# First post-norm of the prompt's first half: columns 0 to 256 normed between the projection tiles of columns 256 to 512, with six split weights kept

## The chip, the cores and the metric

One core of a Trainium2 chip runs the whole program. The metric is the device time of one execution in microseconds. TensorE (PE) does the matrix products, and its weight loads (PEld) run beside them. VectorE (DVE), ScalarE (ACT) and GpSimd (POOL) do the elementwise work, and SyncE (SP) issues most of the transfers between HBM and the chip's memory. Products accumulate in PSUM banks; other tiles lie in SBUF. Every engine has its own queue and takes its instructions in the order in which they stand there.

## The reference

One layer of a streaming encoder, for 1024 prompt frames and 32 sample frames (1056 columns together) of width 1024, in float32:

```
h = x * (1 + sc1) + sh1                    # sc1, sh1, g1 ... from silu(c) @ w_ada
mq, mk, mv, mo, mi, mf, fq, fk, fv, ff, gu, gv = split(h @ w_in)
hm = mlstm(mq, mk, mv, mi, mf) ; hf = forgetting_attention(fq, fk, fv, ff)
vn = layer_norm(gv)                        # also an output for the sample frames
hg = gu * (tril(ws) @ vn + bs)             # per chunk of 128 frames
mix = concat(hm, hf, hg) @ w_o
x = layer_norm(ALPHA * x + (1 + g1) * mix, ln1_g, ln1_b)
h = x * (1 + sc2) + sh2
y = (silu(h @ w_gate) * (h @ w_up)) @ w_down
x = layer_norm(ALPHA * x + (1 + g2) * y, ln2_g, ln2_b)
```

The keys, values and gates of the attention and the states of the mLSTM are outputs too.

## The kernel before

**Arithmetic.** Activations lie with the model dimension on the 128 partitions (8 slices, called k) and frames as columns. Each float32 product is made of three matmuls on halves of the operands: high by high (L117), low by high (L118) and high by low (L119). A weight tile is loaded (`raw`), cast on ACT to its high half (`whi`, L105), and subtracted on VectorE for the low half (`wlo`, L106).

**Columns.** Group 0 is frames 0 to 512, group 1 the other 544 columns. The norm of group 0 works on two ranges of it, `MM[0]`: columns 0 to 256 and 256 to 512.

**The stage that matters here** comes after the mLSTM and the prompt's attention for group 0:

1. `wo_mix(0, ...)` loads the mixers' outputs from HBM (`start_dmix`) into `mlstm_al`, casts the high half into `mlstm_ah` on ACT (L997) and leaves the low half in `mlstm_al`. Six slices are asked for before the gMLP's units, the last two after. `wo_res(0)` loads the residual into `wo_z`, one transfer for each of 8 slices.
2. Four `tm_unit` calls compute the gMLP's halves `gv` and `gu`. `evac_gv` norms `gv` and stores it to HBM (`start_dvn`); a spatial product (L723) takes it back as `tm_gvn`. The gMLP's output is transposed on PE into one bank of the pool `tm_g` (L731) and copied out by ACT as `tm_gms` (L733). Two kinds of FoX unit share PE's `g` banks with it: `fm_unit` computes the attention's queries and keys for one head (`fm_g`, evacuated at L366, L367 and L368 into `fm_qkh`, `fm_qkl`, `fm_qkr`).
3. `wo(0, st, (cut,), ...)` runs once for each range: 8 output tiles (m), each of 8 slices by three matmuls 128x256. Each run loads, casts and splits its own 8 weights. `sublayer_end` evacuates a tile at L1046 on VectorE; `less()` (L1041, POOL) takes off a pivot, the first tile's column mean; `ln_sum` adds the tile into `wo_zs` on POOL (L939) and its square, made by ACT, into `wo_qs` on VectorE (L941).
4. Then `ln1` norms range 0 and after it range 1: two matmuls sum `wo_zs` and `wo_qs` over the partitions (L951), some short VectorE instructions make the scale r and the shift e (L960 to L973), and for each slice there are a multiply (L1063), an add (L1064, on POOL for two of eight), ACT's scale and shift into `lna_tmp` (L1067), ACT's cast into `mlstm_ah` (L1071), and VectorE's low half (L1072). These halves are the operands of the feed-forward's up projection (`up_g`).
5. The last FoX units follow, then `ln1_res` scales the normed residual on POOL (L1081), and the sample's attention `fox_sample` (`foxs_...`, L908 for its output) and the up projections begin.

**What sets the order.** The code is written in this order, but a scheduler places every instruction by a simulated timeline, so instructions of the last FoX units and of the first up projection stand between those of the two norms. A tile waits for its buffer: a pool with n buffers of one tag lets n be alive. PE's accumulators `tm_g`, `fm_g`, `wo_g` and the first `up_g` come from one pool of three banks. `mlstm_ah` and `mlstm_al` of group 0 lie in tiles `ah` and `al` of the pool `ph`; the modulated input of group 0 lies in tiles of its own, `start_h1h` and `start_h1l`, in the pool `p1a`, which is closed (`s6`) once the last FoX unit that reads group 0 has run.

## Time and profile before

| | |
|---|---|
| median of 3 runs | 1378.0 us (1377.67 to 1381.36) |
| profiled execution | 1383.65 us, span of its trace 1381.0 us |
| mean granted TensorE clock | 0.991 |
| gMLP units, first FoX units | up to about 378 us |
| output projection of group 0 (`wo_g`), its matmuls | 378.5 to 425.2 us |
| norms of its two ranges (their sums over partitions, to the last low half) | 425.3 to 471 us |
| group 1, feed-forward, final norms | to the end |

Times in the trace count from the start of its span. A row of the timeline gives start, length, engine, line, operation, output and inputs, and in brackets how long the engine had been idle and what ended it. In a timeline row the length of a matmul includes its way through the pipeline, so rows overlap. In the table of stretches the columns are the stretch, its length, the busy time (and the instructions) of PE, of weight loads, VectorE, ACT and POOL, the granted TensorE clock as a share of full speed, the mean busy share of the 16 DMA engines, and GB/s.

### The profile page before, as it was taken

To read this page: it belongs to the slowest core of one execution; us is meant where nothing else is said; L and a number is where in the kernel's file an instruction comes from. 1 tells how busy PE (TensorE), PEld (TensorE's weight loads), DVE (VectorE), ACT (ScalarE), POOL (GpSimd) and SP (SyncE) were. 2 spreads that over 40 slices of the span, in tenths; PEclk is the share of its full clock that TensorE was granted. 3 is DMA by queue.
4 is the path that set the end of the run, shared out by engine and by line. 5 is a ranking of instruction groups with operands and counts; after the bars stand their busy time and mean duration, and the time that the engine had idled before them with its cause. 6 is when DMAs were issued, how large, how long until landed. Compare 5 with 4: busy or idle time off the path is not lost.

```text
span 1381.0 us, 25237 instructions
## 1 busy us (share of the span) xinstructions
PE 1340.4 (97%) x9432; PEld 1222.8 (89%) x9432; DVE 1008.3 (73%) x2144; ACT 653.7 (47%) x1274; POOL 242.6 (18%) x272
## 2 busy tenths in 40 slices
PE   7999999999899799999999999999999999999996
PEld 4898889889899678888887889899999999999996
DVE  5545654688678757777776766668998988888777
ACT  3314454444445444545544455435564554545355
POOL 0202000033167400000000000264610000000341
PEclk9999999999999999999999999999999999999999
DMA  9765554554764765553443433664597768463321
GB/s 362 261 234 152 162 187 151 175 160 121 244 185 143 212 178 157 139 144 117 135 121 101 105 116 96 192 176 128 156 238 194 206 160 221 131 176 119 98 90 65
DMA packets 123545, 224.65 MB, mean 163 GB/s; under 512 B 21292, under 2 KB 66264, under 8 KB 123424
## 3 DMA queue, kind: packets, MB, share of 16 engines
q1 hardware_dynamic: 117984, 212.75, 49.9%
q0 software_dynamic: 5296, 10.16, 4.7%
q8 instruction: 74, 1.21, 0.4%
q14 instruction: 47, 0.39, 0.1%
q10 hardware_dynamic: 144, 0.14, 0.0%
HBM read 191.21 MB, written 51.72 MB: 176 GB/s over the span
## 4 chain that ended last, share of the span: by engine, by line
PE 84%; DVE 8%; DMA 3%; ACT 2%; issue 1%; POOL 0%; SPq 0%; DVEq 0%; ACTq 0%; POOLq 0%
PE up_g L117 5%; PE up_g L118 5%; PE up_g L119 5%; PE dn_g L119 4%; PE dn_g L117 4%; PE dn_g L118 4%; PE sup_u L119 3%; PE sup_u L117 3%; PE sup_u L118 3%; PE tm_g L283 2%; PE tm_g L282 2%; PE tm_g L284 2%; PE wo_g L119 2%; PE wo_g L117 2%; PE wo_g L118 2%; PE fox_t L818 2%
## 5 line engine op out<-in xcount | busy, mean ns | idle before, releaser
L117 PE MATMUL up_g<-mlstm_ah,up_whi 128*128 128x512 f32 (+1 forms) x384 | 141.8, 370 | 5.0 <-ACT lna_tmp L1067 3.3
L118 PE MATMUL up_g<-mlstm_al,up_whi 128*128 128x512 f32 (+1 forms) x384 | 142.2, 370 | 0.6 <-DVE mlstm_al L1072 0.6
L119 PE MATMUL up_g<-mlstm_ah,up_wlo 128*128 128x512 f32 (+1 forms) x384 | 141.3, 368 | 0.0
L283 PE MATMUL tm_g<-tm_wlo,start_h1h 128*128 128x256 f32 (+1 forms) x384 | 109.5, 286 | 0.9 <-DVE tm_wlo L106 0.9
L282 PE MATMUL tm_g<-tm_whi,start_h1h 128*128 128x256 f32 (+1 forms) x384 | 109.4, 287 | 0.2 <-DVE tm_traw L352 0.2
L284 PE MATMUL tm_g<-tm_whi,start_h1l 128*128 128x256 f32 (+1 forms) x384 | 109.3, 286 | 0.0
L1191 ACT CAST sup_whi<-sup_raw 128x1024 fp32r<-128x1024 f32 x54 | 56.0, 1047 | 90.7 <-PE dn_u L118 47.2
L117 PEld LDWEIGHTS up_g<-mlstm_ah,up_whi 128*128 128x128 f32 x384 | 73.4, 191 | 17.3 <-ACT mlstm_ah L1071 3.5
L118 PEld LDWEIGHTS up_g<-mlstm_al,up_whi 128*128 128x128 f32 x384 | 73.5, 191 | 12.4 <-DVE up_actl L1125 0.8
L119 PEld LDWEIGHTS up_g<-mlstm_ah,up_wlo 128*128 128x128 f32 x384 | 73.7, 192 | 10.8
L791 ACT ACTIVATE fox_p<-fox_s,fox_fmx 128x384 f32<-128x384 f32 (+2 forms) x96 | 55.2, 579 | 56.4 <-DVE fox_fmx L789 43.4
L105 ACT CAST up_whi<-up_raw 128x1024 fp32r<-128x1024 f32 x50 | 52.4, 1048 | 60.8 <-PE dn_g L118 20.6
L1046 DVE SCALAR_TENSOR_TENSOR wo_z<-dn_g,start_mod,wo_z 128x512 f32<-128x512 f32 (+4 forms) x120 | 60.2, 520 | 22.2 <-PE dn_g L119 21.5
L1192 DVE TENSOR_TENSOR sup_wlo<-sup_raw,sup_whi 128x1024 fp32r<-128x1024 f32 x54 | 68.1, 1265 | 10.8 <-ACT sup_whi L1191 10.8
L283 PEld LDWEIGHTS tm_g<-tm_wlo,start_h1h 128*128 128x128 f32 x384 | 72.2, 188 | 2.5 <-issue 1.2
L282 PEld LDWEIGHTS tm_g<-tm_whi,start_h1h 128*128 128x128 f32 x384 | 72.1, 189 | 2.1 <-issue 0.8
L106 DVE TENSOR_TENSOR up_wlo<-up_raw,up_whi 128x1024 fp32r<-128x1024 f32 x50 | 66.6, 1333 | 9.6 <-ACT up_whi L105 8.9
L117 PE MATMUL dn_g<-up_acth,dn_whi 128*128 128x512 f32 (+2 forms) x200 | 73.5, 368 | 0.0
L118 PE MATMUL dn_g<-up_actl,dn_whi 128*128 128x512 f32 (+2 forms) x200 | 73.3, 368 | 0.0
L119 PE MATMUL dn_g<-up_acth,dn_wlo 128*128 128x512 f32 (+2 forms) x200 | 73.3, 366 | 0.0
L284 PEld LDWEIGHTS tm_g<-tm_whi,start_h1l 128*128 128x128 f32 x384 | 72.2, 188 | 0.9 <-issue 0.8
L105 ACT CAST dn_whi<-dn_raw 128x1024 fp32r<-128x1024 f32 (+1 forms) x44 | 42.7, 971 | 50.6 <-PE up_g L118 11.3
(643 smaller groups left out, 4606.0 us busy)
## 6 DMA issues: line engine op xcount, KB each, us to landing
up_raw<-w_gu SPq DMA_DIRECT2D x50, 512.0 KB
dn_raw<-w_dn SPq DMA_DIRECT2D x28, 512.0 KB
ada_late<-w_ada SPq DMA_DIRECT2D x24, 512.0 KB
wo_raw<-w_o SPq DMA_DIRECT2D x24, 512.0 KB
sup_raw<-w_gu SPq DMA_DIRECT2D x20, 512.0 KB
start_dp<-w_gu SPq DMA_DIRECT2D x19, 512.0 KB
start_dp<-w_gu POOLq DMA_DIRECT2D x19, 512.0 KB, 7.7
sup_raw<-start_dp SPq DMA_DIRECT2D x18, 512.0 KB
```

Source lines behind the costliest of these rows:

```text
L105: nc.scalar.copy(hi[:, :w], raw[:, :w])
L106: (eng or nc.vector).tensor_tensor(lo[:, :w], raw[:, :w], f(hi[:, :w]), ALU.subtract)
L117: nc.tensor.matmul(ps, hi, xh(k), start=start and k == 0, stop=False)
L118: nc.tensor.matmul(ps, hi, xl(k), start=False, stop=False)
L119: nc.tensor.matmul(ps, lo, xh(k), start=False, stop=stop and k == n - 1)
L282: nc.tensor.matmul(ps[:, :ncol], xh, hi, start=k == 0, stop=False)
L283: nc.tensor.matmul(ps[:, :ncol], xh, lo, start=False, stop=False)
L284: nc.tensor.matmul(ps[:, :ncol], xl, hi, start=False, stop=k == 7)
L791: nc.scalar.activation(pr[:, lo:hi], banks[x][:, :hi - lo], AF.Exp, bias=mxs[:, 0:1], accum_out=sums[:, x:x + 1])
L1046: self.lastz = self.nc.vector.scalar_tensor_tensor(z[:, m, x:y], ps[:, x - a:y - a], g[i], z[:, m, x:y], ALU.mult, ALU.add)
L1191: nc.scalar.copy(h, x)
L1192: tt(l, x, f(h), ALU.subtract)
```

## The change

1. Group 0's projection is split. `wo_range` does range 0's eight tiles; then range 1's tiles are made in the order 0, 5, 6, 7, 3, 4, 1, 2, and woven with `ln1` of range 0: one slice of the norm for one tile in the text. The norm of range 1 follows.
2. Six of the eight split weights stay in SBUF for range 1: 0, 1 and 2 in a pool of their own (`pw`), 5, 6 and 7 in the pool where they were made. Weights 3 and 4 are loaded and split again.
3. `ln_begin(nc.vector)`: the sums into `wo_zs` are made on VectorE. The adds of group 0 for k = 1 and 5 (L1064) too.
4. One place for two operands: group 0's modulated input now lies in the same tiles `ah` and `al` that later hold the mixers' outputs; `p1a` and `s6` are gone, and a slice of the mixers' outputs can be loaded once the last reader of the input's slice there is done.
5. `wo_res` loads the residual in two transfers of 1 MB instead of eight of 256 KB.
6. Stores leave SP's queue: the `gv` rows (`start_dvn`, 9 of them) and the keys `o_kT` go to POOL's queue; for the heads after the norm `o_kT` goes to ACT's queue, and the key itself and the sample's queries and keys are made by ACT instead of POOL.
7. The sample's attention output takes 12 matmuls of 32x64 for each group of heads instead of 24 of 64x32, then a copy, a transposing matmul and a copy; its stores, now two for each group, are on ACT's queue.
8. Smaller buffers make room: one `mixs` buffer instead of two, `tmres` in `tmsum`'s place, narrower `late` and kept weights.

```
-    def weights(self, src, nk, ncol, eng=None):
+    def weights(self, src, nk, ncol, eng=None, pool=None):
+        pool, width = (pool, 1024) if pool else (self.wp, 1056)
...
-        self.store(self.dvn[:n, tt, :], v[:n])
+        self.store(self.dvn[:n, tt, :], v[:n], nc.gpsimd)
...
-            nc.gpsimd.tensor_tensor(kr[:, :n], f(hi[:, :n]), f(lo[:, :n]), ALU.add)
+            if act:
+                nc.scalar.activation(kr[64:, :n], ps[64:], AF.Copy)
+            else:
+                nc.gpsimd.tensor_tensor(kr[:, :n], f(hi[:, :n]), f(lo[:, :n]), ALU.add)
...
-            self.store(self.d["o_kT"][h, :, o:o + n], kr[64:, :n])
+            self.store(self.d["o_kT"][h, :, o:o + n], kr[64:, :n], nc.scalar if act else nc.gpsimd)
...
-            for x in range(4):
-                for b in range(3):
-                    nc.tensor.matmul(o[r, oc], vv, pT[:w, b, 32 * x:32 * x + 32], start=b == 0, stop=b == 2)
+            for b in range(3):
+                for x in range(4):
+                    nc.tensor.matmul(o[32 * x:32 * x + 32, 0:64], pT[:w, b, 32 * x:32 * x + 32],
+                                     vc[:, b, h] if b < 2 else self.vs[:, h], start=b == 0, stop=b == 2)
+            nc.scalar.copy(ob, o[:, 0:64])
+            nc.tensor.transpose(o[0:64, P:2 * P], ob, self.ident)
...
-        for k in range(KT):
-            self.load(z[:, k], self.d["xT"][k, :, GO[c]:GO[c] + GN[c]])
+        for k in range(0, KT, 4):
+            self.load(z[:, k:k + 4], self.d["xT"][k:k + 4, :, GO[c]:GO[c] + GN[c]].rearrange("k p n -> p k n"))
...
+    def wo_range(self, st, a, b, order, kept, pool):
+        nc, ko = self.nc, self.KORDER
+        hh, hl = self.hh[0][a], self.hl[0][a]
+        st["order"] = order
+        for m in order:
+            self.phase = "wo0"
+            w = kept.get(m) or self.weights(self.d["w_o"][m], KT, P, None, pool if m < 3 else None)
+            kept[m] = w
+            ps = self.t(self.pg, [P, 512], F32, "g")
+            self.gemm(ps[:, :b - a], [w[k] for k in ko], slice(0, P), lambda i: hh[:, ko[i], :b - a],
+                      lambda i: hl[:, ko[i], :b - a])
+            self.sublayer_end(0, self.z[0], m, ps, "g1", st, a, b)
+            yield
...
-            (nc.gpsimd if k % 4 == 1 else nc.vector).tensor_tensor(zk, zk, e, ALU.add)
+            (nc.gpsimd if c and k % 4 == 1 else nc.vector).tensor_tensor(zk, zk, e, ALU.add)
...
-        self.h1t = [[self.t(p, [P, KT, n], F32R, x) for x in ("h1h", "h1l")] for p, n in zip((p1a, self.p1), GN)]
+        self.h1t = [self.wide_tiles(), [self.t(self.p1, [P, KT, GN[1]], F32R, x) for x in ("h1h", "h1l")]]
...
-        st = self.ln_begin(nc.gpsimd)
-        for cut in MM[0]:
-            self.wo(0, st, (cut,), nc.vector)
-        self.operand(0, self.ph)
-        for a, b in MM[0]:
-            weave(self.ln1(0, st, a, b))
+        st = self.ln_begin(nc.vector)
+        with ExitStack() as s7:
+            pw = self.pool("pw", ctx=s7)
+            kept = {}
+            weave(self.wo_range(st, *MM[0][0], range(KT), kept, pw))
+            del kept[3], kept[4]
+            weave(self.wo_range(st, *MM[0][1], (0, 5, 6, 7, 3, 4, 1, 2), kept, pw), self.ln1(0, st, *MM[0][0]))
+        weave(self.ln1(0, st, *MM[0][1]))
         for h in range(PRE, 8):
-            self.fm_unit(w3[2 + h], self.evac_qk(h), (1,))
+            self.fm_unit(w3[2 + h], self.evac_qk(h, True), (1,))
```

**Where the instructions go.** In the rows below, a name's number tells its instance, `x8` means that many alike in a row, and lines of the kernel after stand a little higher: L1063 becomes L1088, L1064 L1089, L1046 L1071, L951 L960, L939 L948.

TensorE before, at the end of the projection: the rows `wo_g_5400` are the last tile of range 1, and `wo_zs_4836`, `wo_qs_4837` are range 0's sums.

```order
L119 MATMUL wo_g_5400<-mlstm_ah_3907,wo_wlo_5397 128x256
L117 MATMUL wo_g_5400<-mlstm_ah_3907,wo_whi_5396 128x256
L118 MATMUL wo_g_5400<-mlstm_al_3908,wo_whi_5396 128x256
L119 MATMUL wo_g_5400<-mlstm_ah_3907,wo_wlo_5397 128x256
L951 MATMUL lna_t_5431<-wo_zs_4836,start_onesm_138 128x256
L951 MATMUL lna_t_5433<-wo_qs_4837,start_onesm_138 128x256
L117 MATMUL fm_g_5559<-start_h1h_171,fm_whi_5555 128x272
```

TensorE after, at the third tile (`wo_g_5203`) of range 1, whose weight halves `wo_whi_5050` and `wo_wlo_5051` are kept ones:

```order
L119 MATMUL wo_g_5166<-mlstm_al_3901,wo_whi_5013 128x256
L120 MATMUL wo_g_5166<-mlstm_ah_3900,wo_wlo_5014 128x256
L118 MATMUL wo_g_5203<-mlstm_ah_3900,wo_whi_5050 128x256
L933 MATMUL wo_t_5148<-wo_z_755_3920,start_ones_45_140 128x256
L960 MATMUL lna_t_5153<-wo_zs_4820,start_onesm_138 128x256
L119 MATMUL wo_g_5203<-mlstm_al_3901,wo_whi_5050 128x256
L120 MATMUL wo_g_5203<-mlstm_ah_3900,wo_wlo_5051 128x256
```

The sums of range 0 now stand between the matmuls of range 1's third tile, and not behind its eighth.

VectorE before, where range 0's norm begins (`lna_tmp_5435` and `wo_pv_4838` are the statistics of range 0, `wo_g_5400` is the last projection tile):

```order
L1046 SCALAR_TENSOR_TENSOR wo_z_759_3927<-wo_g_5400,start_mod_156,wo_z_759_3927 128x256
L106 TENSOR_TENSOR fm_wlo_5706<-fm_raw_5703,fm_whi_5705 128x1024
L941 TENSOR_TENSOR wo_qs_4837<-wo_qs_4837,wo_tmp_5427 128x256
L970 SCALAR_TENSOR_TENSOR lna_tmp_5435<-lna_t_5433,start_epsa_117,lna_tmp_5435 128x256
L960 SCALAR_TENSOR_TENSOR lna_tmp_5435<-lna_tmp_5435,wo_pv_4838 128x256
L367 SCALAR_TENSOR_TENSOR fm_qkl_5585<-fm_g_5559,start_qsc_147,fm_qkh_5584 128x272
L961 TENSOR_TENSOR lna_tmp_5435<-lna_tmp_5435,wo_pv_4838 128x256
L962 SCALAR_TENSOR_TENSOR wo_pv_4838<-lna_tmp_5435,wo_pv_4838 128x256
L973 SCALAR_TENSOR_TENSOR wo_qs_4837<-lna_t_5431,wo_pv_4838 128x256
L1063 TENSOR_TENSOR wo_z_759_3927<-wo_z_759_3927,wo_pv_4838 128x256 x8
L1064 TENSOR_TENSOR wo_z_759_3927<-wo_z_759_3927,wo_qs_4837 128x256 x3
```

VectorE after, in the middle of range 1's projection (`wo_g_5240`, `wo_g_5283` and `wo_g_5326` are its fourth, fifth and sixth tiles):

```order
L1071 SCALAR_TENSOR_TENSOR wo_z_755_3920<-wo_g_5240,start_mod_156,wo_z_755_3920 128x256
L970 TENSOR_TENSOR lna_tmp_5157<-lna_tmp_5157,wo_pv_4822 128x256
L948 TENSOR_TENSOR wo_zs_4820<-wo_zs_4820,wo_z_755_3920 128x256
L971 SCALAR_TENSOR_TENSOR wo_pv_4822<-lna_tmp_5157,wo_pv_4822 128x256
L107 TENSOR_TENSOR fm_wlo_5508<-fm_raw_5505,fm_whi_5507 128x1024
L982 SCALAR_TENSOR_TENSOR wo_qs_4821<-lna_t_5153,wo_pv_4822 128x256
L1088 TENSOR_TENSOR wo_z_755_3920<-wo_z_755_3920,wo_pv_4822 128x256 x8
L1071 SCALAR_TENSOR_TENSOR wo_z_755_3920<-wo_g_5283,start_mod_156,wo_z_755_3920 128x256
L1089 TENSOR_TENSOR wo_z_755_3920<-wo_z_755_3920,wo_qs_4821 128x256
L107 TENSOR_TENSOR fm_wlo_5583<-fm_raw_5580,fm_whi_5582 128x1024
L1089 TENSOR_TENSOR wo_z_755_3920<-wo_z_755_3920,wo_qs_4821 128x256 x5
```

All eight multiplies of range 0's norm now stand ahead of the evacuation of range 1's fifth tile, and the adds around it and the sixth's.

ScalarE before, at the copy `tm_gms` that frees a bank of PE:

```order
L105 CAST wo_whi_4841<-wo_raw_4839 128x1024
L997 CAST mlstm_ah_3907<-mlstm_al_3908 128x512 x3
L733 COPY tm_gms_4627<-tm_g_4560 128x512
L997 CAST mlstm_ah_3907<-mlstm_al_3908 128x512
L714 COPY tm_vhl_4651<-tm_tmres_4649 32x256
```

ScalarE after:

```order
L1008 CAST mlstm_ah_3900<-mlstm_al_3901 128x512
L106 CAST wo_whi_4828<-wo_raw_4826 128x1024
L106 CAST wo_whi_4865<-wo_raw_4863 128x1024
L106 CAST fm_whi_4730<-fm_raw_4728 128x1024
L296 COPY tm_tmsum_4633<-tm_g_4616 32x256
L1008 CAST mlstm_ah_3900<-mlstm_al_3901 128x512 x2
L740 COPY tm_gms_4613<-tm_g_4546 128x512
```

Two casts of the mixers' outputs instead of three stand right ahead of that copy; the casts of two projection weights stand further ahead of it.

More of the change, by code (lines that the diff above doesn't have):

```diff
@@ L175, in ada @@
         for half in range(2):
-            raw = self.t(pool, [P, 1056], F32, tag, bufs)[:, :1024]
+            raw = self.t(pool, [P, 1024 if tag == "late" else 1056], F32, tag, bufs)[:, :1024]
             self.load(raw, self.d["w_ada"][u, :, half * 1024:(half + 1) * 1024])
@@ L974, in ln_stats, with wide_tiles @@
         return r, e
+    def wide_tiles(self):
+        return [self.t(self.ph, [P, KT * 544], F32R, x, 1)[:, :KT * 512].rearrange("p (k n) -> p k n", k=KT)
+                for x in ("ah", "al")]
     KORDER = (2, 3, 4, 5, 0, 1, 6, 7)
@@ L982, in operand @@
             if 0 not in self.hh:
-                tile = lambda tag: self.t(pool, [P, KT * 544], F32R, tag, 1)[:, :KT * 512].rearrange(
-                    "p (k n) -> p k n", k=KT)
-                self.hh[0], self.hl[0] = ({0: x, 256: x[:, :, 256:]} for x in (tile("ah"), tile("al")))
+                self.hh[0], self.hl[0] = ({0: x, 256: x[:, :, 256:]} for x in self.wide_tiles())
             return
@@ L1343, in run @@
         self.constants()
[L1344 removed]
+        self.ph = self.pool("ph")
+        s1 = ExitStack()
         self.p1 = self.pool("p1", ctx=s1, side="right")
         self.sm = self.pool("sm", 2, ctx=s1, side="right")
[L1347 to L1348 removed]
+        self.h1t = [self.wide_tiles(), [self.t(self.p1, [P, KT, GN[1]], F32R, x) for x in ("h1h", "h1l")]]
         self.hs = self.t(self.p1, [P, KT, 2 * NS], F32R, "hs")
```

36 lines of the change are left out of this document (17 added, 19 removed).

## The prediction

> **What bounds the kernel now.** I read the page's list of busy time first.
>
> ```profile
> span 1381.0 us, 25237 instructions
> PE 1340.4 (97%) x9432; PEld 1222.8 (89%) x9432; DVE 1008.3 (73%) x2144; ACT 653.7 (47%) x1274; POOL 242.6 (18%) x272
> ```
>
> TensorE is busy for 97% of the span; VectorE is busy enough to become late in a stage, POOL is not. A change that leaves the matmuls alone, as this nearly does, is worth only what TensorE waits, and what its clock loses. So next come the waits of TensorE in the stage around the change, 330 to 480 us (columns: waited for, us in total, times, longest), and then the granted clock (before the last two columns) in the stretches behind the waits.
>
> ```profile
> PE up_g L117 <- ACT lna_tmp L1067: 3.3, 1, 3.3
> PE fm_g L117 <- ACT tm_gms L733: 2.6, 1, 2.6
> PE ada_g L179 <- DVE up_sil L1123: 1.9, 1, 1.9
> PE up_g L117 <- DVE fm_qkl L367: 1.3, 1, 1.3
> PE wo_g L117 <- ACT tm_gms L733: 0.9, 1, 0.9
> PE up_g L118 <- DVE mlstm_al L1072: 0.6, 1, 0.6
> PE up_g L117 <- DVE ada_adam L187: 0.3, 1, 0.3
> ```
>
> ```profile
> 365.00:371.00 6.00, 6.00 (x29) 6.00 (x29) 1.63 (x4) 1.53 (x4) 0.76 (x1) 0.52 1.00 356
> 400.00:420.00 20.00, 20.00 (x168) 19.95 (x167) 17.12 (x22) 9.58 (x16) 13.03 (x12) 1.00 0.59 179
> 463.00:467.00 4.00, 3.89 (x21) 3.89 (x22) 2.48 (x7) 3.99 (x11) 4.00 (x8) 0.59 0.46 167
> 470.00:474.00 4.00, 4.00 (x31) 2.98 (x24) 1.66 (x6) 0.37 (x1) 0.00 (x0) 0.61 1.04 208
> ```
>
> The projection (400 to 420 lies in it) runs at full clock, 168 matmuls in 20 us or 0.119 us each. On both sides of it lie two holes. Place A, around 364: 2.6 us of waiting, then a stretch that loses 6.0 x (1 - 0.52) = 2.9 us, 5.5 together. Place B, 451 to 476: the five waits on lna_tmp, up_sil, fm_qkl, mlstm_al and ada_adam, 3.3 + 1.9 + 1.3 + 0.6 + 0.3 = 7.4 us, and 4 x 0.41 + 4 x 0.39 = 3.2 us of lost clock, 10.6 together. Some 16 us are therefore to be had, and not more.
>
> Why A waits is in the timelines of TensorE, ScalarE and SP's queue.
>
> ```profile
> 364.58 0.60 PE L117 MATMUL fm_g<-start_h1h,fm_whi 128*128 128x272 f32 x1 [2.62 <-ACT tm_gms L733]
> ```
>
> ```profile
> 358.93 0.62 ACT L997 CAST mlstm_ah<-mlstm_al 128x512 fp32r<-128x512 f32 x1 [2.79 <-DMA mlstm_al<-start_dmix]
> 361.32 1.04 ACT L105 CAST wo_whi<-wo_raw 128x1024 fp32r<-128x1024 f32 x1
> 362.26 1.65 ACT L997 CAST mlstm_ah<-mlstm_al 128x512 fp32r<-128x512 f32 x3
> 363.94 0.59 ACT L733 COPY tm_gms<-tm_g 128x512 f32<-128x512 f32 x1
> ```
>
> ```profile
> 355.16 2.71 SPq L87 DMA_DIRECT2D mlstm_al<-start_dmix  x6
> 357.91 6.23 SPq L87 DMA_DIRECT2D wo_z<-xT  x8
> ```
>
> The copy that frees PE's bank starts at 363.94, behind a weight cast and three casts of mixer outputs, and the first of these casts itself stood 2.79 us waiting for its load. Those six loads leave SP only at 355.16, with the residual's eight right behind them.
>
> Why B waits is in VectorE's rows for the two norms.
>
> ```profile
> 428.48 0.47 DVE L970 SCALAR_TENSOR_TENSOR lna_tmp<-lna_t,start_epsa,lna_tmp 128x256 f32<-128x256 f32 x1
> ...
> 448.56 0.47 DVE L970 SCALAR_TENSOR_TENSOR lna_tmp<-lna_t,start_epsa,lna_tmp 128x256 f32<-128x256 f32 x1
> ```
>
> The first norm's statistics begin at 428.48, the second's only at 448.56, 20 us later; the waits at B are TensorE standing until the second delivers.
>
> **The change part by part.** The sum is made against the profiled execution, 1383.65 us, which lies 5.65 above the median of 1378.0; I take the difference for both and subtract it from the median.
>
> *The weave of norm and projection.* The sums over partitions of range 0 move from behind all 192 matmuls of range 1 to behind 49 of them: 143 x 0.119 = 17 us earlier. VectorE isn't free then, so what counts is when it has done both jobs. Its prices are in its groups for 376 to 475 us (instructions, busy us, mean ns), with those of POOL behind.
>
> ```profile
> L106 DVE TENSOR_TENSOR wo_wlo<-wo_raw,wo_whi 128x1024 fp32r<-128x1024 f32 x14 | 19.9, 1423 | 7.3 <-ACT wo_whi L105 7.3
> L941 DVE TENSOR_TENSOR wo_qs<-wo_qs,wo_tmp 128x256 f32<-128x256 f32 x14 | 11.5, 822 | 0.0
> L1063 DVE TENSOR_TENSOR wo_z<-wo_z,wo_pv 128x256 f32<-128x256 f32 x16 | 7.8, 558 | 0.0
> L1046 DVE SCALAR_TENSOR_TENSOR wo_z<-wo_g,start_mod,wo_z 128x256 f32<-128x256 f32 x16 | 7.6, 474 | 2.1 <-PE wo_g L119 1.6 <-POOL wo_z L1041 0.5
> L1072 DVE TENSOR_TENSOR mlstm_al<-lna_tmp,mlstm_ah 128x256 fp32r<-128x256 f32 x16 | 6.8, 467 | 1.3 <-ACT mlstm_ah L1071 1.3
> L106 DVE TENSOR_TENSOR fm_wlo<-fm_raw,fm_whi 128x1024 fp32r<-128x1024 f32 x4 | 5.5, 1380 | 0.2 <-ACT fm_whi L105 0.2
> L1064 DVE TENSOR_TENSOR wo_z<-wo_z,wo_qs 128x256 f32<-128x256 f32 x12 | 4.4, 412 | 0.0
> ...
> L1081 POOL TENSOR_SCALAR wo_z<-wo_z,start_colp 128x256 f32<-128x256 f32 x16 | 16.2, 1017 | 2.7 <-ACT lna_tmp L1067 2.7
> L1041 POOL TENSOR_TENSOR wo_z<-wo_z,wo_pv 128x256 f32<-128x256 f32 x14 | 14.5, 1071 | 10.0 <-ACT wo_pv L925 10.0
> L939 POOL TENSOR_TENSOR wo_zs<-wo_zs,wo_z 128x256 f32<-128x256 f32 x12 | 14.3, 1188 | 3.9 <-DVE wo_z L1046 3.3
> ```
>
> In range 1's projection VectorE now has 8 evacuations (3.8), 2 weight splits of `wo` and 3 of FoX (2 x 1.42 + 3 x 1.38 = 7.0), some 6 short ones for pivot and statistics (at the 0.47 of L970, 2.8), 4 sums of z and 2 of squares (at 0.41 to 0.82 each, middle 3.7), 8 multiplies (4.5), 8 adds (3.3) and 2 low halves (0.9): 26 us, against 192 x 0.119 = 22.9 us of TensorE. It is about 3 late at the end. The eight multiplies (4.5 us) stand ahead of the fifth tile's evacuation, and the banks hold three tiles, so TensorE is caught in the projection: a new wait of 3 us (0 if VectorE's own slack carries it, 6 if each square keeps its 0.82), with half a microsecond of clock, so 3.5. The second norm then starts when VectorE has done the remaining six low halves (2.8 us) and its lateness (3), not a whole norm (20) behind the first; less the sums and squares it still owes (2), about 12 us are gained, more than B's 7.4 us of waits. I therefore take all of B, 10.6, less 3.5: -7.
>
> *Six splits less.* VectorE loses 6 x 1.42 = 8.5 us, ScalarE six casts (1.04 each in the row at 361.32), SP six loads of 512 KB. ScalarE and the transfers are beside TensorE either way; VectorE's part is in the 26 us above. No term of its own.
>
> *Sums on VectorE.* 14 adds leave POOL. On VectorE I bound one by two rows of its like, the first made beside a POOL add of the same kind, the second with POOL idle:
>
> ```profile
> 401.51 0.95 DVE L941 TENSOR_TENSOR wo_qs<-wo_qs,wo_tmp 128x256 f32<-128x256 f32 x1
> ...
> 404.75 0.41 DVE L941 TENSOR_TENSOR wo_qs<-wo_qs,wo_tmp 128x256 f32<-128x256 f32 x1
> ```
>
> That makes +5.7 to +13.3 us, against the 8.5 saved. With POOL rid of these adds, the squares' 0.82 should fall towards 0.41 also (14 x 0.41 = 5.7 us back). Net about zero, on an engine that is late only in range 1, where it is counted. The four L1064 adds are 4 x 0.41 = 1.6 us, counted too.
>
> The row at 401.51 is told more sharply by the Trainium skill, "SBUF — State Buffer", section "SBUF: two separate sides": VectorE with two SBUF inputs and GpSimd exclude each other from a shared port pair for the whole instruction. The trace agrees with 0.95 against 0.41; by the rule every add of squares beside POOL would pay, and moving the sums to VectorE takes half of the meetings away, which would put the 26 us nearer 24 and the sum at -12.
>
> *One operand place.* The mixer loads now stand on SP in pieces ahead of the residual, and have to wait for the last reader of the old operand's slice. Two casts stand right before the tm_gms copy instead of three, and two weight casts have gone further ahead. If the loads land while ScalarE has other work, A's 5.5 is gone; if they land later than now, it is kept or grows by a cast or two (2 x 0.62). I take -4 (0 to -5.5). The 0.9 us before the first wo_g stay: that copy still ends the gMLP.
>
> *The residual in two transfers* shortens SP's queue by most of 6.23 us; it is needed at 378, so nothing hangs on it: 0. *Stores off SP*: 9 and some `o_kT` issues leave a queue that isn't waited for, 0, but see the rivals. *Keys on ScalarE*: 8 + 4 short instructions on an engine with 47% busy, 0 (up to +1 if one stands ahead of an lna_tmp).
>
> *The sample's output.*
>
> ```profile
> L908 PE MATMUL foxs_o<-foxs_pth,foxs_v x32: 222/223/243, 500.3 to 510.2; 128*64 128x32 f32 x32
> ```
>
> 24 small matmuls for each group become 12 with twice the columns, and a copy and a transpose between; TensorE goes on with up tiles meanwhile. 0 (-0.8 to +1.5). Smaller buffers: 0 (up to +1).
>
> Sum: -7 - 4 = -11 us: span 1370, profiled execution 1372.6, median 1367. The best end is -10.6 - 5.5 - 0.8 = -17, 1361; the worst of this forecast has the new wait at 6 with 2 of clock, A kept, and foxs_o at +1.5: -10.6 + 8 + 1.5 = -1, 1377.
>
> One rule of the Trainium skill bears on the clock's part: "TensorE: Matmul & The Clock Gate", section "Part 1: The HAM clock gate (the "warmup" mystery)", ties the slow clock to an idle window of about 3.4 us. Here 0.52 followed a gap of only 2.62 us and 0.61 one of 1.86, so the trace shows less idling to suffice; by the page only the 3.33 us gap would cost clock, and the sum would be about -8 instead of -11.
>
> **The rivals.** *R1: VectorE's lateness eats B.* For it: 26 us against 22.9, and eight multiplies ahead of an evacuation. Against it: POOL is lighter. The wait is 6 and a slow stretch takes 3, so B yields 1.6 and A 4: 1372.
>
> *R2: the gv stores arrive late from POOL's queue.* On SP a store and the load that takes it back were 1.75 us apart; the transfers issued from POOL elsewhere land after 5.0 to 5.9.
>
> ```profile
> 292.01 0.33 SPq L91 DMA_DIRECT2D start_dvn<-tm_traw  x1
> 293.76 0.33 SPq L87 DMA_DIRECT2D tm_gvn<-start_dvn  x1
> ...
> DMA to landing us min/median/max: 5.0/5.2/5.9
> ...
> 335.38 0.75 POOL L354 TENSOR_TENSOR tm_traw<-tm_traw,start_rowp 128x256 f32<-128x256 f32 x1
> ...
> 347.61 0.38 PE L723 MATMUL tm_g<-tm_gvn,start_wsp 128*128 128x128 f32 x1
> ```
>
> For the rows finished at 336.1: issue 0.6, landing 5.9, load back 2 gives 344.6, where TensorE wants them at 347.6, and some 4 us earlier in the new order. So it is 3 in hand or 1 short; a wait of 1 to 4 with its slow stretch eats A's 4 us: 1371 to 1373, say 1372. The Trainium skill, in the same section as above, warns that a transfer issued from GpSimd's queue starves while VectorE holds the shared pair; no run here shows that yet.
>
> *R3: the gain is given back.* TensorE arrives earlier at the next load: at 470 to 474 the transfer engines are already full (1.04). What it wins it would wait there: 1378.
>
> *R4, slower: POOL holds VectorE up.* In range 1 and the norms VectorE has 62 two-input instructions more exposed (7 sums of z, 7 of squares, 3 x 16 of the norms), each 0.54 dearer beside POOL (0.95 - 0.41): 33 us times the share s that meets POOL's work. It breaks even with the 11 us at s = 1/3, is over +0.3% from 0.46 and at 0.7 gives +12: 1390. Against it: POOL loses the 14.3 us of its sums, a part of s is in the means of now already (0.558 and 0.822), and L1064 kept 0.412 although POOL's scalings fall among the norms.
>
> **How the numbers follow.** The forecast (-17 to -1) gets 0.50, R1 0.13, R2 0.12, R3 0.10, R4 0.15. A measurement of this kernel tells about 0.3% (4.1 us) from no change: 1373.9 to 1382.1. Faster: most of the forecast (0.46), R1 and R2 with 0.12 and 0.11: 0.69. Within: the tails of these and most of R3, 0.13. Slower: R4 and a part of R3, 0.18. The range reaches from 1359 (the best end and the runs' own spread of 2) to 1382, which takes in R1 to R3 and leaves R4 out.
>
> **What would show it.** The waits on lna_tmp and up_sil in place B gone or under 1 us each, and the clock there near 1.0; the wait on tm_gms under 1; the second norm's first L970 (at 448.56 now) about 12 us nearer to the last wo_g; adds of z on VectorE near 0.45. R1 shows as a wait of wo_g on L1046 (L1071 then), R2 as one on tm_gvn, R3 as new waits on transfers beyond 470, R4 as L1063 and L1064 near 0.9. I am wrong if VectorE's two-input instructions stay dear or if the mixer loads land late in their new place.

## The result

The changed kernel takes 1378.42 us (median of 12 runs, 1374.64 to 1382.22), the kernel before 1379.84 us (12 runs, 1377.15 to 1381.4). The ratio is 0.9990, 95% interval 0.9980 to 1.0001. Forecast were 1367 us and a range of 1359 to 1382: the time lies in the range, but no gain clear of noise came.

The page of the changed kernel, its list of busy time:

```profile
span 1376.5 us, 25170 instructions
PE 1335.4 (97%) x9434; PEld 1215.7 (88%) x9434; DVE 998.5 (73%) x2156; ACT 653.3 (47%) x1282; POOL 225.2 (16%) x259
```

TensorE's waits in the changed kernel, 345 to 478 us first, then 478 to 906 us (waited for, us in total, times, longest):

```profile
PE fm_g L118 <- ACT tm_gms L740: 2.4, 1, 2.4
PE up_g L118 <- DVE up_sil L1147: 1.4, 1, 1.4
PE up_g L118 <- ACT start_qks L378: 1.0, 1, 1.0
PE wo_g L118 <- ACT tm_gms L740: 0.3, 1, 0.3
...
PE fox_s L789 <- ACT fox_p L798: 4.0, 3, 2.4
PE wo_g L118 <- ACT up_ah L1016: 2.6, 1, 2.6
PE fox_s L789 <- ACT foxs_pth L906: 1.0, 1, 1.0
PE foxs_s L890 <- DMA foxs_k<-start_dsf: 0.2, 1, 0.2
```

Before, the second stretch held two waits only:

```profile
PE fox_s L782 <- ACT fox_p L791: 1.1, 1, 1.1
PE fox_t L818 <- DVE fox_p L799: 0.2, 1, 0.2
```

So place B went from 7.4 us of waits to 2.4, and behind 478 us the waits rose from 1.3 to 7.8. The table adds the waits up by stage, each kernel in two profiles (the second ones are the first two experiments), and beneath them what the slow clock lost ahead of the end of the program (a slow stretch's length times the share of the clock that was not granted). The sums count every idle gap, also the short ones that the lists leave out.

| us | before | before, again | after | after, again |
|---|---|---|---|---|
| waits 280 to 345 | 4.9 | 5.0 | 4.1 | 5.6 |
| waits at A, 345 to 379 | 3.5 | 3.3 | 2.8 | 2.4 |
| waits at B, 425 to 478 | 7.4 | 6.0 | 2.4 | 2.4 |
| waits 478 to 560 | 0.0 | 0.0 | 2.9 | 2.7 |
| waits 560 to 906 | 1.3 | 1.5 | 5.0 | 4.2 |
| slow clock at A and B | 6.8 | 5.1 | 0.0 | 1.7 |
| slow clock elsewhere | 1.7 | 0.0 | 3.4 | 0.0 |
| span | 1381.0 | 1377.2 | 1376.5 | 1374.9 |

A and B together fell from a mean of 16.1 us to 5.9. The other four rows rose from a mean of 7.2 to 14.0. The spans before and after differ by the remaining 3.4 us in the mean, the timed runs by 1.4. So waits and clock explain the whole difference. TensorE's busy time less the slow clock of the table did not fall: 1340.4 - 8.5 = 1331.9 us and 1337.0 - 5.1 = 1331.9 before, 1335.4 - 3.4 = 1332.0 and 1332.7 - 1.7 = 1331.0 after.

VectorE's groups of the changed kernel for 376 to 475 us show that its instructions became cheaper:

```profile
L107 DVE TENSOR_TENSOR wo_wlo<-wo_raw,wo_whi 128x1024 fp32r<-128x1024 f32 x7 | 9.1, 1301 | 4.6 <-PE lna_t L960 3.3 <-ACT wo_whi L106 1.3
L950 DVE TENSOR_TENSOR wo_qs<-wo_qs,wo_tmp 128x256 f32<-128x256 f32 x14 | 7.1, 508 | 0.3
L1089 DVE TENSOR_TENSOR wo_z<-wo_z,wo_qs 128x256 f32<-128x256 f32 x16 | 5.9, 419 | 0.0
L1088 DVE TENSOR_TENSOR wo_z<-wo_z,wo_pv 128x256 f32<-128x256 f32 x16 | 5.5, 417 | 0.0
L948 DVE TENSOR_TENSOR wo_zs<-wo_zs,wo_z 128x256 f32<-128x256 f32 x12 | 5.3, 441 | 0.2
```

The squares' adds fell from 822 to 508 ns, the multiplies from 558 to 417, and the sums that came from POOL take 441. TensorE does not wait once in the projection. VectorE was late all the same. Here are the projection's last matmul, the evacuations of range 1's seventh and last tiles, and the start of the second norm's statistics:

```profile
424.04 0.28 PE L120 MATMUL wo_g<-mlstm_ah,wo_wlo 128*128 128x256 f32 x1
...
426.96 0.47 DVE L1071 SCALAR_TENSOR_TENSOR wo_z<-wo_g,start_mod,wo_z 128x256 f32<-128x256 f32 x1
...
427.68 0.47 DVE L1071 SCALAR_TENSOR_TENSOR wo_z<-wo_g,start_mod,wo_z 128x256 f32<-128x256 f32 x1
...
437.24 0.48 DVE L979 SCALAR_TENSOR_TENSOR lna_tmp<-lna_t,start_epsa,lna_tmp 128x256 f32<-128x256 f32 x1
```

The evacuations of the last four tiles start 4.0, 4.7, 5.4 and 3.4 us after their tile's last matmul has ended. A tile takes TensorE 2.9 us. With three banks two more tiles can be made meanwhile, 5.8 us, less the 0.5 that the evacuation takes itself: the lateness just fits in. The seventh tile's evacuation ends at 427.43, and the product that is third behind it starts at 427.48. The second norm starts 13.2 us behind the last matmul, where it was 448.56 - 425.17 = 23.4 before.

### The profile page after: what moved, and what is told of

It is laid out like the page before. It is cut to its first block, busy times and chain, and to the rows that moved or that the text cites. A ratio compares the mean times of both kernels' runs of the same rounds, so it can differ in the third digit from the quotient of the medians.

```text
span 1376.5 us, 25170 instructions
## 1 busy us (share of the span) xinstructions
PE 1335.4 (97%) x9434; PEld 1215.7 (88%) x9434; DVE 998.5 (73%) x2156; ACT 653.3 (47%) x1282; POOL 225.2 (16%) x259
## 4 chain that ended last, share of the span: by engine, by line
PE 63%; DMA 5%; DVE 5%; ACT 1%; issue 1%; SPq 0%; ACTq 0%; DVEq 0%
PE up_g L118 5%; PE up_g L120 5%; PE up_g L119 5%; PE dn_g L118 4%; PE dn_g L120 4%; PE dn_g L119 4%; PE sup_u L120 3%; PE sup_u L118 3%; PE sup_u L119 3%; PE sup_g L119 2%; PE sup_g L120 2%; PE sup_g L118 2%; PE wo_g L118 2%; PE dn_u L118 2%; PE wo_g L120 2%; PE dn_u L119 2%
## 5 line engine op out<-in xcount | busy, mean ns | idle before, releaser
L1071 DVE SCALAR_TENSOR_TENSOR wo_z<-dn_g,start_mod,wo_z 128x512 f32<-128x512 f32 (+4 forms) x120 | 60.3, 521 | 13.4 <-PE dn_g L120 13.0
L830 ACT CAST fox_pth<-fox_t 128x512 fp32r<-128x512 f32 (+1 forms) x80 | 41.0, 544 | 51.9 <-PE fox_t L825 51.8
L831 DVE TENSOR_TENSOR fox_ptl<-fox_t,fox_pth 128x512 fp32r<-128x512 f32 (+1 forms) x80 | 49.5, 631 | 16.7 <-ACT fox_pth L830 16.5
L107 DVE TENSOR_TENSOR dn_wlo<-dn_raw,dn_whi 128x1024 fp32r<-128x1024 f32 (+1 forms) x44 | 49.5, 1126 | 15.8 <-ACT dn_whi L106 15.5
L793 DVE TENSOR_REDUCE fox_fmx<-fox_s 128x1 f32<-128x384 f32 (+2 forms) x96 | 52.7, 553 | 10.1 <-PE fox_s L790 9.1
L283 PE MATMUL tm_g<-tm_whi,start_ah 128*128 128x256 f32 (+1 forms) x192 | 55.1, 290 | 0.0
L283 PE MATMUL tm_g<-tm_whi,start_h1h 128*128 128x256 f32 (+1 forms) x192 | 54.8, 286 | 0.3 <-DVE tm_traw L353 0.2
```

Of the source, the lines that this page charges most:

```text
L107: (eng or nc.vector).tensor_tensor(lo[:, :w], raw[:, :w], f(hi[:, :w]), ALU.subtract)
L283: nc.tensor.matmul(ps[:, :ncol], xh, hi, start=k == 0, stop=False)
L793: nc.vector.tensor_reduce(mxs[:, x:x + 1], s[:, :w], AX.X, ALU.max, negate=True)
L831: nc.vector.tensor_tensor(pl[:, :e], ps[:, :e], f(ph[:, :e]), ALU.subtract)
L1071: self.lastz = self.nc.vector.scalar_tensor_tensor(z[:, m, x:y], ps[:, x - a:y - a], g[i], z[:, m, x:y], ALU.mult, ALU.add)
```

## The experiments

All lines are those of each kernel's own text. Ratios are to the kernel before, timed in the same batch, with their 95% intervals. Medians of different batches are compared by their ratios.

**1. Both kernels profiled once more.** No edit.

> The kernel before, unchanged, profiled once more. Two theories on why the profiled spans differ by 4.5 us and the medians by 1.4: (chance) the slow-clock windows of before's first profile (17.1 us of them ahead of the tail, 8.5 us lost) are an unlucky draw; then this profile shows the same waits of TensorE (about 27 us in all, 7.4 of them between 451 and 477 us) and fewer slow windows, a span near 1377. (fixed) both waits and slow windows come again at 364, 463 and 470, span 1380 to 1382.

> The changed kernel, unchanged, profiled once more and timed against before. Theory G (the gain is given back by the order): the waits behind 480 us (fox_s at 488, 495, 522, 743: 5.0 us; wo_g on up_ah at 892: 2.6 us) come again, each within 1 us. Theory N (they are chance): they differ by more than half, and their sum falls under 4 us in this profile. Either way ratio to before 0.997 to 1.001.

Before, again: 1379.82 us in its one run, span 1377.2. The waits are those of the first profile (27.0 us against 27.5, counting those over a quarter of a microsecond; B has 6.0 instead of 7.4), the slow stretches are not (10.2 us of them instead of 17.1 ahead of the end). That is the expectation's first theory, chance. After, again: 1377.88 us, ratio 0.9986 (0.9974 to 0.9998). Its waits behind 478 us:

```profile
PE fox_s L789 <- ACT fox_p L798: 4.0, 4, 1.5
PE wo_g L118 <- ACT up_ah L1016: 2.5, 1, 2.5
PE fox_t L825 <- DVE fox_p L806: 0.2, 1, 0.2
```

The wait on up_ah is the same to a tenth, those on fox_p have the same sum in other places; 6.7 us where chance would have left under 4. Theory G's first half holds: these waits belong to the kernel. The clock's part is a draw. The stretch 363 to 371 in before, before again, after and after again (the granted clock is the third number from the end):

```profile
363.00:371.00 8.00, 6.42 (x29) 6.42 (x30) 3.63 (x6) 3.50 (x7) 0.76 (x1) 0.57 1.01 362
363.00:371.00 8.00, 5.91 (x36) 5.91 (x37) 4.42 (x8) 4.56 (x10) 0.76 (x1) 0.79 1.02 365
363.00:371.00 8.00, 5.57 (x46) 5.11 (x46) 5.33 (x12) 4.17 (x8) 1.31 (x2) 1.00 0.96 345
363.00:371.00 8.00, 5.60 (x36) 5.11 (x34) 4.55 (x7) 3.83 (x8) 1.31 (x2) 0.79 0.96 340
```

With waits of 2.6, 2.4, 2.4 and 2.4 us there, the clock lost 8 x 0.43 = 3.4, 8 x 0.21 = 1.7, 0 and 1.7 us.

**2. The weave undone, and the weave alone.** The first kernel is the changed one with both norms after range 1:

```
-            weave(self.wo_range(st, *MM[0][1], (0, 5, 6, 7, 3, 4, 1, 2), kept, pw), self.ln1(0, st, *MM[0][0]))
-        weave(self.ln1(0, st, *MM[0][1]))
+            weave(self.wo_range(st, *MM[0][1], (0, 5, 6, 7, 3, 4, 1, 2), kept, pw))
+        weave(self.ln1(0, st, *MM[0][0]))
+        weave(self.ln1(0, st, *MM[0][1]))
```

> The change with the weave alone undone: range 1's tiles first, then both norms one after the other. Theory G: the waits between 450 and 477 us return (6 to 8 us, with 1.7 to 3.4 us of slow clock), and those behind 480 fall from 7.6 back to about 2, so that the time is as before: ratio 0.999 to 1.003. Theory P (the weave is worth 8 us by itself and other parts of the change cost 7): the waits behind 480 stay at 7 to 8, and the ratio is 1.004 to 1.008.

1379.93 us, ratio 1.0002 (0.9989 to 1.0016). Its waits from 445 to 906 us:

```profile
PE up_g L118 <- ACT start_qks L378: 1.9, 1, 1.9
PE up_g L118 <- DVE up_sil L1147: 1.8, 1, 1.8
PE up_g L118 <- ACT fm_qkr L370: 0.5, 1, 0.5
...
PE fox_s L789 <- ACT fox_p L798: 2.7, 1, 2.7
PE wo_g L118 <- ACT up_ah L1016: 2.1, 1, 2.1
PE fox_t L825 <- DVE fox_p L806: 0.2, 1, 0.2
```

Without the weave B waits 4.3 us, against a mean of 6.7 before: of the 4.3 us of waits that the change took from B, 2.4 went without it. Of the waits behind, those of 478 to 560 us are gone, and those on fox_p at 745 and on up_ah are not, 5.0 us where theory G had about 2. Theory G had the time right, but only part of the giving back is the weave's.

The second kernel is the one before with only this, and a `wo_range` of its own that loads and splits every weight again:

```
-        for cut in MM[0]:
-            self.wo(0, st, (cut,), nc.vector)
-        self.operand(0, self.ph)
-        for a, b in MM[0]:
-            weave(self.ln1(0, st, a, b))
+        weave(self.wo_range(st, *MM[0][0], range(KT)))
+        weave(self.wo_range(st, *MM[0][1], range(KT)), self.ln1(0, st, *MM[0][0]))
+        weave(self.ln1(0, st, *MM[0][1]))
```

> The kernel before with the weave alone: range 0's norm between range 1's tiles, all eight weights loaded and split again, sums on POOL, stores where they were. Theory G: the waits between 450 and 477 us fall to 2 to 4 and waits behind 480 rise to 5 to 8, ratio 0.998 to 1.002. Theory P: the waits fall, nothing rises, ratio 0.992 to 0.996. A third way: without the kept weights VectorE is late in range 1 and TensorE waits for a bank there, 3 us or more on L1046.

1386.14 us, ratio 1.0045 (1.0032 to 1.0059), slower than all else. Its waits from 378.6 to 478 us, and the first of those behind 560:

```profile
PE wo_g L119 <- DVE wo_wlo L106: 3.0, 2, 1.8
...
PE up_g L117 <- DVE up_sil L1135: 3.1, 1, 3.1
PE up_g L118 <- DVE mlstm_al L1085: 0.5, 1, 0.5
...
PE wo_g L117 <- ACT up_ah L1005: 3.0, 1, 3.0
```

This is the third way of the expectation in another form: VectorE is late in range 1 (the fifth and sixth tiles' evacuations start 6.3 and 6.6 us after their matmuls), and TensorE waits 3.0 us, for a weight's low half and not for a bank. A wait like rival R1's exists then, where the weights are not kept and POOL still adds. The wait on up_ah has come here too, in a kernel that shares only the weave with the changed one.

**3. The order at the end of the mixers.** In the timelines of TensorE, the last fox_o row and the first row of group 1's projection, before, and after with the row that waits:

```profile
867.58 0.28 PE L831 MATMUL fox_o<-fox_pth,fox_v 128*128 128x256 f32 x1
...
894.59 0.29 PE L117 MATMUL wo_g<-up_ah,wo_whi 128*128 128x272 f32 x1
```

```profile
872.04 0.28 PE L838 MATMUL fox_o<-fox_pth,fox_v 128*128 128x256 f32 x1
...
886.47 0.29 PE L118 MATMUL wo_g<-up_ah,wo_whi 128*128 128x272 f32 x1
...
892.20 0.39 PE L118 MATMUL wo_g<-up_ah,wo_whi 128*128 128x272 f32 x1 [2.56 <-ACT up_ah L1016]
```

Before, TensorE had 27.0 us of other work between the last attention output and the projection that reads it; after, 14.4. Of 62 down-projection matmuls that stood in between before, the scheduler has left 8 there. The experiment puts them behind the output again:

```
-                    nc.tensor.matmul(o[:, q], v[:, b, :], ph[:, c], start=False, stop=full > 1 and b == order[-1])
+                    self.lasto = nc.tensor.matmul(o[:, q], v[:, b, :], ph[:, c], start=False,
+                                                  stop=full > 1 and b == order[-1])
...
-                self.gemm(p[:, :b - a], w, slice(m % 2 * P, m % 2 * P + P), lambda k: act[j0 + k][0][:, a:b],
-                          lambda k: act[j0 + k][1][:, a:b])
+                with self.tc.issue_after(self.lasto.ins) if m >= hold else ExitStack():
+                    self.gemm(p[:, :b - a], w, slice(m % 2 * P, m % 2 * P + P), lambda k: act[j0 + k][0][:, a:b],
+                              lambda k: act[j0 + k][1][:, a:b])
...
-                self.down(0, g, act, WIDE, st)
+                self.down(0, g, act, WIDE, st, hold=3)
```

> The changed kernel with one order restored at the end of the mixers: from the fourth output tile on, group 0's down projection (dn_g) stands on TensorE behind the last matmul of the prompt's attention (fox_o), as it did before the change (60 of its matmuls there, 8 in the changed kernel). Nothing else differs. Theory O (the wait of wo_g on up_ah, 2.5 us in two profiles, is the order's: too little work is left behind the last fox_o to cover store, load and cast of the last mixer outputs): that wait falls under 0.5 us, none over 1 us takes its place, ratio to before 0.9960 to 0.9975, that is 2 to 2.5 us below the changed kernel. Theory C (the mixers' chain has its own pace, and TensorE waits for it wherever the filler stands): the wait moves to fox_t or fox_o between 845 and 875, 2 us or more, ratio 0.998 to 0.999.

1375.83 us, ratio 0.9971 (0.9958 to 0.9984). From 845 to 906 us TensorE has one row of waits left:

```profile
PE fox_o L833 <- DVE fox_ptl L831: 1.3, 2, 0.8
```

The 2.5 us on up_ah are gone, 1.3 us stand among the last attention outputs. That is theory O with a part of C: half of the wait's size, in two waits of at most 0.8, comes back where the filler was taken from. This kernel is faster than before clear of noise; against the changed kernel's 0.9986 it is 2 us lower, but the two intervals overlap.

The other profiles say the same. With 8 down-projection matmuls in between, or none (after, twice, e_serial, e_weave, e_gms_vector, e_zs_pool), TensorE waits 2.1 to 3.0 us on up_ah. With 38 or more (before, twice, 38 in e_fo_old and e_fo_new, 60 in e_join and the three kernels built on it) it does not wait there at all.

**4. Place A.** The copy that frees the gMLP's bank, moved from ScalarE to VectorE:

```
-        nc.scalar.copy(s[:, :, :nt, :n], ps[:, :, :nt, :n])
+        nc.vector.tensor_copy(s[:, :, :nt, :n], ps[:, :, :nt, :n])
```

> The changed kernel with the copy tm_gms, which frees the gMLP's bank, on VectorE instead of ScalarE. Theory Q (place A is ScalarE's queue: the copy stands behind casts of weights and of mixer outputs that themselves wait for loads): the wait of fm_g at 366 (2.4 us in both profiles) falls under 1 us. Rival: the transposes ahead of the copy are what is late, then it stays at 2 us or more. Time 1 to 3 us below the changed kernel by Q, ratio 0.996 to 0.998.

1378.0 us, ratio 0.9991 (0.9977 to 1.0004). Its waits from 280 to 379 us on that copy:

```profile
PE tm_g L283 <- DVE tm_gms L740: 1.1, 1, 1.1
...
PE wo_g L118 <- DVE tm_gms L740: 1.3, 1, 1.3
PE fm_g L118 <- DVE tm_gms L740: 0.6, 1, 0.6
```

Theory Q holds for the place: fm_g's wait falls from 2.4 to 0.6 us, so ScalarE's queue was the cause. Its time did not come, since the copy is now late twice elsewhere: the three waits on it make 3.0 us, where the changed kernel had 2.4 and 0.3. What ScalarE did ahead of the copy in the changed kernel (its timeline):

```profile
360.36 0.62 ACT L1008 CAST mlstm_ah<-mlstm_al 128x512 fp32r<-128x512 f32 x1 [2.31 <-DMA mlstm_al<-start_dmix]
360.89 1.99 ACT L106 CAST wo_whi<-wo_raw 128x1024 fp32r<-128x1024 f32 x2
362.79 1.04 ACT L106 CAST fm_whi<-fm_raw 128x1024 fp32r<-128x1024 f32 x1
363.86 0.36 ACT L296 COPY tm_tmsum<-tm_g 32x256 f32<-32x256 f32 x1
364.37 1.27 ACT L1008 CAST mlstm_ah<-mlstm_al 128x512 fp32r<-128x512 f32 x2 [0.15 <-DMA mlstm_al<-start_dmix]
365.67 0.59 ACT L740 COPY tm_gms<-tm_g 128x512 f32<-128x512 f32 x1
```

One cast waited 2.31 us for its mixer load, as one had waited 2.79 before, and the two weight casts came to stand right behind it.

**5. The sums back on POOL.** `self.ln_begin(nc.gpsimd)` for group 0, the rest as changed.

> The changed kernel with the sums of z for group 0 back on POOL. If POOL's two-input adds hold VectorE up: VectorE's adds of squares go from a mean of 508 ns to 650 or more, its multiplies (417 ns) to 500 or more, and waits of 1 us or more return between 400 and 477; ratio 1.000 to 1.003. If they don't: VectorE has 14 x 0.44 = 6 us less to do, ratio 0.997 to 0.999.

1383.11 us, ratio 1.0024 (1.0011 to 1.0037). VectorE's groups for 376 to 475 us:

```profile
L950 DVE TENSOR_TENSOR wo_qs<-wo_qs,wo_tmp 128x256 f32<-128x256 f32 x14 | 8.2, 589 | 2.7 <-ACT wo_tmp L944 2.6
L1088 DVE TENSOR_TENSOR wo_z<-wo_z,wo_pv 128x256 f32<-128x256 f32 x16 | 6.7, 489 | 0.0
```

Both are dearer beside POOL's adds (589 against 508, 489 against 417), though less than the expectation's bounds. TensorE waits 0.4 us in the projection and 0.3 right behind it for evacuations (L1071), which start 5.5 and 5.8 us after their tiles' matmuls: the banks' slack is used up. None of the expected waits of 1 us came there or at B, where TensorE waits only 0.9 us in all. And yet the kernel is 4.7 us slower than the changed one (0.9990): 5.5 us of waits between 478 and 560 us, 2.8 on `mlstm_mixs` at 759 and 3.0 on up_ah. This run says it most plainly: B all but empty, and the time worse.

**6. The sample's attention output.** The changed kernel with the old product:

> The changed kernel with the old output product of the sample's attention (24 matmuls for each group, one store on SP's queue). If the new form causes the waits of fox_s at 488 to 523 us (2.5 us in both profiles): they fall under 0.5. If the late weight loads on SP's queue cause them, with ScalarE held at a cast: they stay at 1.5 to 3 us. One profile can't tell 1 us in the total time.

1379.41 us in one run. The waits of fox_s between 478 and 560 us fall from 2.7 to 0.3 us, as the first branch asks, but one of 2.2 us on foxs_k stands at 480, ahead of the place; the stage's sum (2.5) is near the changed kernel's 2.9 and 2.7. It doesn't tell the new form from the late loads. For the loads speaks ScalarE's timeline in the changed kernel, with TensorE's row behind it:

```profile
493.80 1.04 ACT L106 CAST up_whi<-up_raw 128x1024 fp32r<-128x1024 f32 x1 [5.00 <-DMA up_raw<-w_gu]
494.75 0.57 ACT L798 ACTIVATE fox_p<-fox_s,fox_fmx 128x384 f32<-128x384 f32 x1
...
495.47 0.45 PE L789 MATMUL fox_s<-fox_k,fox_qp 128*128 128x384 f32 x1 [0.93 <-ACT fox_p L798]
```

ScalarE stands 5 us at a cast whose weights have not landed, the softmax is behind it in its queue, and TensorE behind the softmax.

The kernel before with the new product alone, its loops, copies and stores included:

```
-                    nc.tensor.matmul(o[r, oc], vv, pT[:w, b, 32 * x:32 * x + 32], start=b == 0, stop=b == 2)
...
+                    nc.tensor.matmul(o[32 * x:32 * x + 32, 0:64], pT[:w, b, 32 * x:32 * x + 32],
+                                     vc[:, b, h] if b < 2 else self.vs[:, h], start=b == 0, stop=b == 2)
...
```

> The kernel before with the new output product of the sample's attention alone. Its matmuls go from 2.15 us to 0.46 us for each group, so TensorE has 3.3 us less to do. If that alone comes through: ratio 0.9970 to 0.9985, waits between 345 and 478 as before. If the new order behind it gives it back: ratio 0.999 to 1.002 and 1.5 us or more of waits on fox_s, foxs_s or wo_g that before hadn't.

1378.81 us, ratio 0.9996 (0.9983 to 1.0009): 0.8 us of the 3.3 in the medians. None of the expected new waits came, but fox_s at 739 waits 2.3 us (1.1 and 1.3 in the two profiles of before), with a slow stretch behind it. Neither branch holds whole. TensorE's busy time less the slow clock is 1336.2 - 6.8 = 1329.4 us, 2.5 under before, and 1339.7 - 5.1 = 1334.6 us in e_fo_old, 3.1 over the mean of the changed kernel: the saving itself is real.

**7. Parts on top of the restored order.** The gv stores back on SP's queue:

> The kernel e_join with the gv stores (start_dvn) back on SP's queue. If those stores land late from POOL's queue (rival R2): the wait of tm_g on the load of tm_gvn at 310 us (1.4 us in x_after2, e_join and e_zs_pool) goes, and the ratio to before is 0.995 to 0.9965, 1 to 2 us below e_join. If the load is late for another reason, or the wait only moves: it stays or another of its size stands between 300 and 345, ratio 0.9965 to 0.998.

1374.95 us, ratio 0.9965 (0.9952 to 0.9979), the lowest median of all kernels here. The 1.4 us on tm_gvn are gone, and 1.9 us on `mlstm_mqk` (which the kernel before has, with 1.6) are back in the same stage, 5.2 us of waits against 5.5. That is the second branch's wait that only moves. R2's late landing is real and costs nothing that can be measured.

The restored order without the weave:

> The kernel e_join without the weave: range 1's tiles, then both norms one after the other. It prices the weave where the order behind it is the same. By the waits (4.3 + 1.7 us of clock without it between 425 and 478, 2.3 with it, but 0.0 against 2.0 to 2.9 between 478 and 560): the weave is worth 0 to 2 us, ratio 0.997 to 0.999. If the weave's gain were only hidden by the order at the end of the mixers: ratio 1.000 or more, 4 us above e_join.

1378.81 us, ratio 0.9996 (0.9980 to 1.0013). In the same comparison as e_join_dvn (0.9965) it is 3.9 us slower, and their intervals do not overlap; the two differ in the gv stores as well. Against e_join (0.9971) it is 3.4 us slower, and the intervals just overlap. B waits 5.0 us in it, against 2.2 in e_join. So the weave is worth some 3 us where the order at the end is held, between the expectation's two branches.

The keys of the last heads on POOL again:

> The kernel e_join_dvn with the keys of the last heads made and stored by POOL again instead of ScalarE. If ScalarE's queue is what is left in place B (up_g waits 0.97 us for start_qks, a small copy on ScalarE): that wait goes, nothing takes its place, ratio to before 0.995 to 0.9965 as in e_join_dvn or 1 us below. If POOL's additions hold VectorE up again: VectorE's multiplies and adds of the norms rise from 417 ns to 450 or more, the waits between 445 and 478 us rise from 2.3 to 4 or more, ratio 0.998 to 1.000.

1376.85 us, ratio 0.9975 (0.9957 to 0.9992), not to be told from e_join_dvn. The 1.0 us on start_qks are gone; 1.7 us on `mlstm_al` and 0.6 and 0.5 us elsewhere have taken its place at B (2.8 against 2.3). The multiplies rose only from 415 to 432 ns, the low halves from 448 to 530.

## Why the prediction was wrong

**The two places: right in sum, partly by luck.** Forecast were -7 at B and -4 at A, 11 us; measured are 16.1 - 5.9 = 10.2 us in the means of two profiles. B gave 6.7 - 2.4 = 4.3 of waits and 3.4 of clock. Its mechanism was right: the wait on lna_tmp is gone, and the second norm starts 10 us nearer to the last matmul, where 12 were forecast. But 2.4 us stayed at B and none came in range 1, where the forecast had 0 and 3.5; the two errors cancel. A gave 0.8 of waits and 1.7 of clock, and neither is the forecast's mechanism: fm_g's wait on tm_gms stayed at 2.4, since a cast still waits for a mixer load ahead of the copy, now 2.31 us. What fell is wo_g's wait of 0.9, which the forecast kept, and the clock is a draw. The forecast's condition for A, loads that land while ScalarE has other work, was not met.

**The new wait in range 1: wrong.** VectorE was late by the forecast's size, 3.4 to 5.4 us in the last four tiles, but TensorE was not caught: "the banks hold three tiles" was read as a limit that 3 us exceed, and it is a slack of two tiles less one evacuation, some 5.3 us. The runs bear this out: no wait to speak of at 5.4 us (after), waits of 0.4 and 0.3 at 5.5 and 5.8 (e_zs_pool). e_weave, with 6.6, waits 3.0 us, but for low halves that came late as well. The sums of the forecast were too high as well. They took the squares at up to 0.82 us, the multiplies at 0.56 and a split at 1.42; measured are 0.51, 0.42 and 1.30.

**The step that failed** is the last one: "Sum: -7 - 4 = -11 us", carried to the end of the program: 11 us were forecast, and the timed medians differ by 1.4. It treats the 900 us behind B as fixed. They are not: the scheduler orders them anew, and the waits outside A and B, with their slow clock, rose from 7.2 to 14.0 us, by 6.8. 2.5 of this is the order at the end of the mixers (e_join takes that wait away), 2.8 are waits of the attention between 478 and 560 us, of which the weave is a condition (none in e_serial and e_join_serial), and the remainder is fox_s near 743 (0.7) and the clock (0.9); 280 to 345 us did not rise. R3 had the result, 1378, and a part of the mechanism, a cast that waits for its weights at 488 to 494; it had a chance of 0.10 and nothing on the order. Which part of the change sets the order at the end of the mixers stays open: the wait on up_ah is in e_weave, which shares only the weave with the changed kernel, and in e_serial, which shares all but the weave; it is in neither e_fo_old nor e_fo_new.

**R1 and R4** did not occur: TensorE has no wait on L1071, and the multiplies and the adds of squares became cheaper. e_zs_pool shows a weak form of both. **R2's** late landing occurred in three profiles (1.4 to 1.5 us on tm_gvn); of the nine stores from POOL's queue in the changed kernel seven landed 1.7 to 3.4 us after their issue and two after 4.9 and 5.6, where R2 had taken 5.9 for all. It was worth nothing that can be measured. By the Trainium skill, "SBUF — State Buffer", section "SBUF: two separate sides", VectorE with two SBUF inputs and GpSimd exclude each other on a shared port pair; the trace agrees in direction. With the place of the sums as the only edit (e_zs_pool against after) the squares take 589 and 508 ns and the multiplies 489 and 417. The rest of their fall, from 822 and 558, has another cause, which no run isolates. What the moved sums took from TensorE's waits on evacuations is 0.7 us, so the prediction's gain of 1 us for this was not too small.

**The sample's output: mis-sized, and misread.** The prediction and the part on the change say that 24 matmuls of a group become 12. That is wrong: the loops make 12 in either form, and the traces show 24 records in either. The stretches with one group's foxs_o alone, after and before (PE busy is the third number):

```profile
493.80:494.60 0.80, 0.68 (x24) 0.42 (x24) 0.00 (x0) 1.00 0.00 0
...
500.30:502.70 2.40, 2.36 (x24) 1.97 (x24) 0.00 (x0) 1.00 0.04 15
```

0.68 us instead of 2.36, for two groups 3.4 us less, where the term was 0 (-0.8 to +1.5). It was the largest saving of TensorE's own work, and it was taken for nothing. In the changed kernel it does not show: TensorE's busy time less the slow clock is 1331.9 us before and 1332.0 and 1331.0 after, so other products took some 3 us more in their new order. This too is a cost that the sum of places left out; which products bear it was not taken apart.

## What to carry to other kernels

Where a scheduler orders the program, a local saving is a forecast of the place, not of the time: compare the order of the queues to the end, above all how much independent work stands between a producer's last instruction and the product that reads it (27.0 us before and 14.4 after here), and price it. An engine that evacuates late costs nothing until its lateness exceeds what the banks cover (two tiles of 2.9 us here, less the evacuation). Look in each queue for what stands behind a transfer: one cast that waits for its weights held the softmax and with it TensorE. And profile the kernel before twice: its slow stretches here differed by 3.4 us between two profiles with nearly the same waits.

## What the runs showed of the hardware

The same wait of about 2.4 us at A cost 3.4, 1.7, 0 and 1.7 us of clock in four profiles. The Trainium skill, "TensorE: Matmul & The Clock Gate", section "Part 1: The HAM clock gate (the "warmup" mystery)", calls the window that decides free-running, about 3.4 us long; the steps of 1.7 us (half of 3.4) and the scatter agree with that, while gaps of 2.4 us, under its full idle window, were enough here. A wait's clock loss was therefore a chance here and not a fixed term. In all fourteen profiles, between 60 us and the end of TensorE's work, each of the eight waits of 3.0 us or more had a slow stretch begin within 2 us of its end, and 16 of the 28 waits between 2 and 3 us had one.

The sample's attention output, with 32x64 results in four places of a bank, took 0.68 us for 24 records, against 2.36 us with 64x32 results in two places, and the arithmetic is the same. What in the form makes the difference (the results' places, the narrower weights, the order of the heads in the loops) was not taken apart.
